# Eighteen constant products at the start of TensorE's program, and six more projection pieces ahead of the first scores

## The chip, the cores and the metric

The kernel runs on one core of a Trainium2 chip. The metric is the device time of one execution in microseconds, as the median of several runs. Lower is better. A core has five engines with a program each, which run side by side and wait for one another by semaphores: TensorE (PE, matrix products; its weight loads are listed apart as PEld), VectorE (DVE), ScalarE (ACT), GpSimd (POOL) and SyncE (SP), which here issues nearly all transfers.

## The reference

One layer of a decoder with 1024 tokens and width 1024. A condition vector gives shifts, scales and gates; the token matrix is modulated, projected, attended in two ways, merged, normalized, and sent through a feed-forward block:

```python
mod = (jnp.einsum('bd,de->be', c_act, w_ada[l]) + b_ada[l])[:, None, :]
shift_m, scale_m, gate_m, shift_f, scale_f, gate_f = jnp.split(mod, 6, axis=-1)
u = x * (1.0 + scale_m) + shift_m
y = mixer(u, positions, w_in[l], sinks[l], w_branch_a[l], w_branch_b[l], w_o[l])
x = layer_norm(DEEPNORM_ALPHA * x + (1.0 + gate_m) * y, ln1_g[l], ln1_b[l])
u = x * (1.0 + scale_f) + shift_f
y = swiglu(u, w_gate_up[l], w_down[l])
x = layer_norm(DEEPNORM_ALPHA * x + (1.0 + gate_f) * y, ln2_g[l], ln2_b[l])
```

The mixer projects `u` by `w_in` (46 column blocks of 128 for queries, keys and values, and 16 for gates), turns queries and keys by rotary tables, runs a sliding-window attention (16 heads) and three dilated attentions (8 heads each), and merges them with sigmoid gates.

## The kernel before

**Tiles.** Everything is float32. Where a large product is needed, each operand is split into a rounded high part and a low rest, and three products (high by high, high by low, low by high; lines 137 to 139) are added up in a PSUM bank of 128 by 512. ACT makes the high part (line 78 for weights, `w_hi`), DVE the rest (line 79, `w_lo`). The modulated input `u` lies in on-chip memory by 8 blocks of 128 features (`k`), two halves of 512 tokens (`t`).

**Prologue** (lines 196 to 367). For each of the 8 feature blocks `j`: the columns of `w_ada` for shift and scale are multiplied by `c_act` and summed over the 1024 condition features. `on_pe[j]` of the 8 partial sums are made by PE (`ada_direct`, line 248, products with one column), the rest by DVE (`ada_sum`, lines 240 and 242, into `acc`). PE then folds `acc` over the partitions with a column of ones (`ada_rest`, line 254). DVE adds the bias (`modulate`, lines 259 and 260, tile `mod`); ACT makes `u` from it (lines 265 and 266), and POOL its low part (line 269). On DVE stands, in this order for every block: `modulate(j)`, `ada_sum(j + 1)`, the low part of an early weight block (line 118), a step of the rotary tables. PE meanwhile multiplies three early weight blocks (blocks 0 to 2; lines 278 and 283) with what there is of `u`. `ones` is a constant of 128 by 128 ones.

**Projection stream and attention** (lines 410 to 775). `stream()` is a generator that yields the projection of blocks 3, 4, ... in pieces: one piece is two feature blocks of one token half, 6 products of 128 by 512; 4 pieces make a half, 8 a column block. A half that is done is taken out of its bank `pj` (two banks) by `evacuate`: for keys and queries DVE does lines 422 and 423 (`ra`, `rb`), POOL lines 425 and 426 (into `r` or `o`); for values ACT copies (line 484). The first attention unit uses the early blocks 0, 1, 2 (key, value, query); blocks 3, 4, 5 are key, value and query of the second unit. After some ticks (one tick a piece, `soon`) a key is split (ACT lines 454 and 455 into `kh`, DVE line 460 into `kl`) and a query likewise (lines 439 and 440, `qs`).

**What sets the order.** The program is written out in one order, and every engine runs its own instructions in that order. The loop at lines 742 to 769 goes over (unit, quarter) steps `s`. Each step issues `scores` (PE lines 501 and 507 into two banks `s`, which the next step uses again; DVE masks and row maxima at lines 513 and 520), pieces up to a count, `turn_probs` of the step before (PE line 550), `exponentials` (ACT line 528), more pieces, and `weigh` (PE line 573). `pump(n)` runs the stream until `n` pieces are done in all. Line 741 is the start: 8 pieces before the first scores; then `at(0.4)`, `at(0.8)` and `at(1.0)` ask for 8, 10 and 12 in step 0, and 14, 16 and 18 in step 1.

Of the kernel before, what the change touches and what calls it, by code (L numbers as in the profile page):

```python
# [10 lines left out]
F32 = mybir.dt.float32  # L11
# [7 lines left out]
P = 128  # L19
# [79 lines left out]
def decoder_layer(ctx: ExitStack, tc: tile.TileContext, I, out, dbg=None):  # L99
    nc = tc.nc  # L100
# [12 lines left out]
    ones = const.tile([P, P], F32, name="ones")  # L113
# [85 lines left out]
    ps_o = ph1.enter_context(tc.tile_pool(name="ps_o", bufs=2, space=PSUM))  # L199
# [18 lines left out]
    with tc.tile_pool(name="pro", bufs=2) as pro:  # L218
# [17 lines left out]
        def ada_sum(j):  # L236

            acc_t[j] = pro.tile([P, 2 * P], F32, name="acc", bufs=2)
            k0 = on_pe[j]
            nc.vector.tensor_scalar(acc_t[j], wa_t[j][:, k0], c_act[:, k0:k0 + 1], None, op0=OP.mult)  # L240
            for k in range(k0 + 1, KC):
                nc.vector.scalar_tensor_tensor(acc_t[j], wa_t[j][:, k], c_act[:, k:k + 1], acc_t[j],
                                               op0=OP.mult, op1=OP.add)

        def ada_direct(j):
            for s in range(2):
                for k in range(on_pe[j]):
                    nc.tensor.matmul(ps_m[:, 2 * j + s:2 * j + s + 1], wa_t[j][:, k, s * P:(s + 1) * P],
                                     c_act[:, k:k + 1], start=(j == 0 and s == 0 and k == 0), stop=False,
                                     skip_group_check=True)  # L250

        def ada_rest(j):
            for s in range(2):
                nc.tensor.matmul(ps_m[:, 2 * j + s:2 * j + s + 1], acc_t[j][:, s * P:(s + 1) * P], ones[:, :1],
                                 start=False, stop=(s == 1), skip_group_check=True)
# [68 lines left out]
        fetch(1)  # L324
        ada_direct(0)
        ada_sum(0)
        ada_rest(0)
        for j in range(KC):
            if j + 2 < KC:
# [41 lines left out]
    def tick():  # L371
        for x in later:
            x[0] -= 1
        for x in [x for x in later if x[0] <= 0]:
            later.remove(x)
            x[1]()
# [326 lines left out]
    ends = np.cumsum(lengths)  # L703
# [3 lines left out]
    def pump(upto):  # L707
        while progress[0] < min(upto, total):
            next(flow)
            progress[0] += 1  # L710
            tick()
# [26 lines left out]

    LEAD = 6
    subs = [(un, qr) for un in units for qr in range(4)]  # L740
    pump(ends[0] + LEAD + 2)
    for s in range(len(subs) + 2):
        n, i = divmod(s, 4)
        start = ends[min(n, len(units) - 1)] + LEAD if n < len(units) else total
        stop = ends[n + 1] + LEAD if n + 1 < len(units) else total
# [555 lines left out]
    f0, ends, nxt = 0, [], 3  # L1301
# [111 lines left out]
```

## Time and profile before

| | us |
|---|---|
| median of 3 runs (1900.1 to 1901.41) | 1901.1 |
| the profiled execution | 1908.77 |
| its span in the trace | 1907.0 |
| PE busy in the span | 1841.1 |
| DVE busy | 1160.4 |
| ACT busy | 782.0 |
| POOL busy | 596.5 |

All moments below are microseconds from the start of the span. The profiled execution was 7.7 us above the median of the timed runs, and 1.77 us of it lie outside the span. PE has work in nearly all of the span; what it lacks lies mostly in the first 100 us. A matmul's length in the trace includes its way through the array, so the pace of a stream is the distance between two starts.

### The profile page before, as it was taken

How to read it: one execution, taken by the hardware profiler on the slowest of the kernel's cores; microseconds unless marked ns; L12 is line 12 of the kernel's file. 1: busy time of each engine (PE TensorE's matmuls, PEld its weight loads, DVE VectorE, ACT ScalarE, POOL GpSimd, SP SyncE). 2: the span in 40 equal slices, each digit the busy share in tenths (PEclk: the TensorE clock that was granted, in tenths of full speed). 3: DMA queues.
4: the chain of work that ended last, by engine and by line, in shares of the span. 5: the costliest groups of instructions: out<-in, count | busy, mean ns of one | idle time of the engine just before them, and what ended most of it. 6: DMA issues, size and time to landing. Idle time of an engine off the chain costs nothing.

```text
span 1907.0 us, 24471 instructions
## 1 busy us (share of the span) xinstructions
PE 1841.1 (97%) x8988; PEld 1489.6 (78%) x8988; DVE 1160.4 (61%) x2161; ACT 782.0 (41%) x1661; POOL 596.5 (31%) x389
## 2 busy tenths in 40 slices
PE   6899999999999999989999999999999999899998
PEld 5688877878878777768888878778888888788886
DVE  7855667667677887534555364575565444565557
ACT  3455545445444767633122132653333333412122
POOL 2432223223323222100311142455664333431213
PEclk9899999999999999989999999999999999999999
DMA  8011112111121122254534123123222222432222
GB/s 316 28 34 34 40 41 74 45 57 56 41 63 50 53 89 68 79 178 164 175 118 161 56 75 124 56 89 100 89 78 89 78 89 95 135 125 90 93 71 89
DMA packets 72266, 170.83 MB, mean 90 GB/s; under 512 B 13073, under 2 KB 14161, under 8 KB 72146
## 3 DMA queue, kind: packets, MB, share of 16 engines
q1 hardware_dynamic: 71810, 168.21, 26.7%
q8 instruction: 71, 1.16, 0.3%
q0 software_dynamic: 336, 1.06, 0.2%
q14 instruction: 49, 0.40, 0.1%
HBM read 145.80 MB, written 23.43 MB: 89 GB/s over the span
## 4 chain that ended last, share of the span: by engine, by line
PE 51%; DVE 3%; ACT 1%; issue 1%; DMA 1%; SPq 0%; POOL 0%; DVEq 0%; ACTq 0%; POOLq 0%
PE pf L1106 21%; PE p L138 5%; PE p L139 5%; PE p L137 5%; PE pf L137 5%; PE pf L139 5%; PE pf L138 5%; DVE m L118 1%; DMA h_raw<-h_d 0%; DVE wd L79 0%; DVE h L118 0%; DMA oa_d<-o 0%; PE px L1034 0%; PE p L835 0%; PE p L842 0%
## 5 line engine op out<-in xcount | busy, mean ns | idle before, releaser
L137 PE MATMUL pj<-u,w_hi 128*128 128x512 f32 x720 | 301.5, 419 | 0.0
L139 PE MATMUL pj<-u,w_lo 128*128 128x512 f32 x720 | 283.9, 394 | 0.0
L138 PE MATMUL pj<-u,w_hi 128*128 128x512 f32 x720 | 282.6, 392 | 0.0
L425 POOL TENSOR_TENSOR rb<-rb,sin_t 128x512 f32<-128x512 f32 x64 | 86.8, 1356 | 502.0 <-DVE rb L423 431.5
L118 DVE TENSOR_TENSOR w_lo<-r,w_hi 128x512 fp32r<-128x512 f32 x110 | 117.7, 1072 | 138.7 <-ACT w_hi L117 137.9
L79 DVE TENSOR_TENSOR w_lo<-w_raw,w_hi 128x512 fp32r<-128x512 f32 x150 | 133.4, 893 | 85.3 <-ACT w_hi L78 83.0
L528 ACT ACTIVATE probs<-probs,st 128x128 f32<-128x128 f32 (+1 forms) x320 | 146.0, 461 | 60.5 <-DVE st L518 30.8
L137 PEld LDWEIGHTS pj<-u,w_hi 128*128 128x128 f32 x720 | 136.4, 189 | 33.6 <-issue 4.7
L139 PEld LDWEIGHTS pj<-u,w_lo 128*128 128x128 f32 x720 | 135.8, 189 | 30.7
L138 PEld LDWEIGHTS pj<-u,w_hi 128*128 128x128 f32 x720 | 136.7, 190 | 22.6
L137 PE MATMUL pf<-wd,h 128*128 128x512 f32 x352 | 139.2, 395 | 3.4 <-DVE zt L1326 2.9
L138 PE MATMUL pf<-wd,h 128*128 128x512 f32 x352 | 138.7, 394 | 1.9 <-DVE wd L79 1.9
L139 PE MATMUL pf<-wd,h 128*128 128x512 f32 x352 | 138.6, 394 | 0.0
L62 POOL TENSOR_TENSOR w_raw<-w_raw,gate 128x512 f32<-128x512 f32 x60 | 83.1, 1404 | 157.0 <-DMA w_raw<-in_w_down 134.4
L1326 DVE SCALAR_TENSOR_TENSOR zt<-zt,pf 128x512 f32<-128x512 f32 x112 | 76.2, 685 | 85.1 <-PE pf L139 85.0
L426 POOL TENSOR_TENSOR r<-ra,rb 128x512 f32<-128x512 f32 x63 | 114.5, 1817 | 6.1 <-DVE kl L460 1.3
L78 ACT ACTIVATE w_hi<-w_raw 128x512 fp32r<-128x512 f32 x150 | 92.0, 624 | 29.0 <-PE p L138 12.0
L552 ACT ACTIVATE ptsb<-pt 128x512 f32<-128x512 f32 (+1 forms) x128 | 63.6, 548 | 93.6 <-PE pt L550 93.2
L137 PE MATMUL p<-u,w_hi 128*128 128x512 f32 x224 | 88.3, 394 | 0.0
L139 PE MATMUL p<-u,w_lo 128*128 128x512 f32 x224 | 87.2, 389 | 0.0
L138 PE MATMUL p<-u,w_hi 128*128 128x512 f32 x224 | 87.2, 389 | 0.0
L137 PE MATMUL p<-o_hl,w_hi 128*128 128x512 f32 x192 | 75.9, 395 | 8.0 <-ACT o_hl L117 8.0
(297 smaller groups left out, 4267.2 us busy)
## 6 DMA issues: line engine op xcount, KB each, us to landing
w_raw<-in_w_in SPq DMA_DIRECT2D x118, 256.0 KB
r<-in_w_gate_up SPq DMA_DIRECT2D x47, 512.0 KB
a_raw<-in_w_ada SPq DMA_DIRECT2D x32, 512.0 KB
w_raw<-in_w_down SPq DMA_DIRECT2D x44, 256.0 KB
h_raw<-h_d SPq DMA_DIRECT2D x22, 512.0 KB
h_d<-g SPq DMA_DIRECT2D x40, 256.0 KB
wa<-in_w_ada_m SPq DMA_DIRECT2D x16, 512.0 KB
wb<-wt_d SPq DMA_DIRECT2D x24, 256.0 KB
```

Source lines behind the costliest of these rows:

```text
L62: self.nc.gpsimd.tensor_tensor(self.raws[i], self.raws[i], scale(), op=OP.mult)
L78: self.nc.scalar.activation(hi, raw, AF.Copy)
L79: self.nc.vector.tensor_tensor(lo, raw, hi, op=OP.subtract)
L118: nc.vector.tensor_tensor(lo, src, hi, op=OP.subtract)
L137: nc.tensor.matmul(ps, w[0], m[0], start=first, stop=False)
L138: nc.tensor.matmul(ps, w[0], m[1], start=False, stop=False)
L139: nc.tensor.matmul(ps, w[1], m[0], start=False, stop=last)
L425: eng.tensor_tensor(b, b, sin_t[:, s], op=OP.mult)
L426: eng.tensor_tensor(residue_half(res, r, t), by_residue(a, r), by_residue(b, r), op=OP.add)
L528: nc.scalar.activation(pr, pr, AF.Exp, bias=st[:, 0, h, b:b + 1], accum_out=st[:, 1, h, b:b + 1])
L1106: nc.tensor.matmul(ps, w[:, c], m[:, k], start=first and k == 0 and n == 0, stop=k == 3 and n == 2, skip_group_check=True)
L1326: nc.vector.scalar_tensor_tensor(z, z, ALPHA if gi == 0 else 1.0, pd, op0=OP.mult, op1=OP.add)
```

## The change

Two edits. At the start of the prologue, between `ada_direct(0)` with `ada_sum(0)` and `ada_rest(0)`, 18 products of `ones` by `ones` are written to a bank of the pool `ps_o`; nothing reads them. And the count of pieces ahead of the first scores goes from 8 to 14. The later counts are the same, so the requests for 8, 10, 12 and 14 pieces then find nothing left to do.

```diff
@@ -324,6 +324,10 @@
         fetch(1)
         ada_direct(0)
         ada_sum(0)
+
+        idle = ps_o.tile([P, P], F32, name="po")
+        for _ in range(18):
+            nc.tensor.matmul(idle, ones, ones, start=True, stop=True)
         ada_rest(0)
         for j in range(KC):
             if j + 2 < KC:
@@ -738,7 +742,7 @@
 
     LEAD = 6
     subs = [(un, qr) for un in units for qr in range(4)]
-    pump(ends[0] + LEAD + 2)
+    pump(ends[0] + LEAD + 8)
     for s in range(len(subs) + 2):
```

In the changed kernel every line from 328 on has a number that is higher by 4 (501 becomes 505, 513 becomes 517, and so on). On PE, at the very start of the program, the difference between the two orders is this; `acc` is the sum that DVE makes, `pt` the bank of the modulation:

```order
-L1409 UNCONDITIONAL_BRANCH
+L1413 UNCONDITIONAL_BRANCH
 L248 MATMUL pt<-c_act,wa 128x1 x8
+L330 MATMUL po<-ones 128x128 x18
 L254 MATMUL pt<-ones,acc 128x1 x4
 L296 MATMUL s<-pos_f,ones 128x512 x2
```

The 18 products stand behind the 8 products of `ada_direct(0)` and ahead of the first `ada_rest`, on which `modulate(0)` waits.

On PE around the first scores, before; `s` are the scores, `pj` the projection, `probs` the masked scores of the first quarter. A line of "..." stands for the products of the pieces between (24 between the two scores, 12 behind the second):

```order
L501 MATMUL s<-kh,qs 128x128 x2
L501 MATMUL s<-kh,qs 128x256 x2
L507 MATMUL s<-kl,qs 128x128 x2
L507 MATMUL s<-kl,qs 128x256 x2
...
L501 MATMUL s<-kh,qs 128x256 x4
L507 MATMUL s<-kl,qs 128x256 x4
...
L550 MATMUL pt<-ident,probs 128x128 x6
```

And in the changed kernel, with nothing left out between them:

```order
L505 MATMUL s<-kh,qs 128x128 x2
L505 MATMUL s<-kh,qs 128x256 x2
L511 MATMUL s<-kl,qs 128x128 x2
L511 MATMUL s<-kl,qs 128x256 x2
L505 MATMUL s<-kh,qs 128x256 x4
L511 MATMUL s<-kl,qs 128x256 x4
L554 MATMUL pt<-ident,probs 128x128 x6
```

The 36 products of six pieces moved ahead of the first scores; the scores of the first two quarters and the turning of the first `probs` now follow each other directly.

On DVE, from the query's split to the first masks, before (`kl` here is the low part of the second unit's key, block 3):

```order
L440 TENSOR_TENSOR qs<-o,qs 64x1024 x2
L422 TENSOR_TENSOR ra<-pj,cos_t 128x512
L423 STREAM_SHUFFLE rb<-pj 128x512
L513 ISA probs,mx<-s,mask 128x128
```

And in the changed kernel:

```order
L444 TENSOR_TENSOR qs<-o,qs 64x1024 x2
L426 TENSOR_TENSOR ra<-pj,cos_t 128x512
L427 STREAM_SHUFFLE rb<-pj 128x512
L464 TENSOR_TENSOR kl<-r,kh 64x1024
L79 TENSOR_TENSOR w_lo<-w_raw,w_hi 128x512
L464 TENSOR_TENSOR kl<-r,kh 64x1024
L79 TENSOR_TENSOR w_lo<-w_raw,w_hi 128x512
L517 ISA probs,mx<-s,mask 128x128
```

Four instructions that stood behind the first masks (the first three of them between the masks of the first and of the second quarter) stand ahead of both now. ACT moved in the same way: the four copies of that key (lines 454 and 455), two `w_hi` and a copy of `vt` stand ahead of the first exponentials instead of behind them.

## Rows read from the trace of the kernel before

**Rows 1.** Page, busy time: us, share of the span, instructions.

```profile
PE 1841.1 (97%) x8988; PEld 1489.6 (78%) x8988; DVE 1160.4 (61%) x2161; ACT 782.0 (41%) x1661; POOL 596.5 (31%) x389
```

**Rows 2.** Stretches: from:to, length, busy by engine (columns in the head), clock, DMA.

```profile
core 0: us, PE busy (x) PEld busy (x) DVE busy (x) ACT busy (x) POOL busy (x), PEclk, DMA share, GB/s
13.00:55.50 42.50, 33.53 (x120) 25.23 (x120) 40.87 (x65) 17.33 (x22) 15.63 (x12) 0.96 0.77 281
70.00:93.00 23.00, 15.81 (x74) 12.68 (x72) 22.45 (x30) 9.87 (x11) 10.50 (x7) 0.87 0.08 24
90.00:100.00 10.00, 8.82 (x29) 6.91 (x30) 7.01 (x16) 4.47 (x11) 3.41 (x2) 0.63 0.00 0
```

**Rows 3.** Timeline, PE at the start: start, length, line, names, count [idle before <-releaser].

```profile
6.43 3.55 PE L248 MATMUL pt<-c_act,wa 128*128 128x1 f32 x16 [6.43 <-DMA wa<-in_w_ada_m]
9.83 0.99 PE L254 MATMUL pt<-ones,acc 128*128 128x1 f32 x4
18.62 1.01 PE L254 MATMUL pt<-ones,acc 128*128 128x1 f32 x4 [7.80 <-DVE acc L242]
```

**Rows 4.** Timeline, DVE in the prologue and behind it.

```profile
10.90 0.16 DVE L259 TENSOR_TENSOR mod<-pt,b_pp 128x2 f32<-128x2 f32 x1 [1.34 <-PE pt L254]
...
12.81 0.35 DVE L240 TENSOR_SCALAR acc<-wa,c_act 128x256 f32<-128x256 f32 x1 [1.55 <-DMA wa<-in_w_ada_m]
...
70.11 0.69 DVE L422 TENSOR_TENSOR ra<-pj,cos_t 128x512 f32<-128x512 f32 x1 [2.56 <-PE pj L283]
```

**Rows 5.** Timeline, later products with a whole float32 operand.

```profile
891.46 0.19 PEld L835 LDWEIGHTS p<-acc,ones 128*128 128x128 f32 x1 [0.24 <-issue]
...
948.13 1.84 PE L842 MATMUL p<-ones,acc 128*128 128x1 f32 x16
```

**Rows 6.** Timeline, PE, two of the early products of the prologue.

```profile
29.35 0.63 PE L278 MATMUL s<-u,e_hi 128*128 128x512 f32 x1
29.78 0.63 PE L278 MATMUL s<-u,e_lo 128*128 128x512 f32 x1
```

**Rows 7.** Timeline, PE around the first two scores.

```profile
83.38 0.39 PE L138 MATMUL pj<-u,w_hi 128*128 128x512 f32 x1
83.61 0.39 PE L139 MATMUL pj<-u,w_lo 128*128 128x512 f32 x1
90.38 0.45 PE L501 MATMUL s<-kh,qs 128*128 128x128 f32 x1 [6.38 <-DVE qs L440]
91.63 0.98 PE L501 MATMUL s<-kh,qs 128*128 128x128 f32 x3 [0.81 <-DVE qs L440]
92.54 0.79 PE L507 MATMUL s<-kl,qs 64*128 64x128 f32 x4
...
97.27 0.46 PE L137 MATMUL pj<-u,w_hi 128*128 128x512 f32 x1
...
104.62 0.81 PE L550 MATMUL pt<-ident,probs 128*128 128x128 f32 x6
105.19 0.48 PE L137 MATMUL pj<-u,w_hi 128*128 128x512 f32 x1
```

**Rows 8.** Timeline, DVE around the first masks.

```profile
92.13 0.72 DVE L423 STREAM_SHUFFLE rb<-pj 128x512 f32<-128x512 f32 x1
93.37 0.29 DVE L513 CUSTOM_DVE_ANT_0 probs<-s,mask 128x128 f32<-128x128 f32 x1 [0.52 <-PE s L507]
...
94.82 1.62 DVE L520 TENSOR_SCALAR st<-mx 128x2 f32<-128x2 f32 x1
98.44 1.22 DVE L460 TENSOR_TENSOR kl<-r,kh 64x1024 fp32r<-64x1024 f32 x1 [2.00 <-ACT kh L454]
100.18 0.69 DVE L79 TENSOR_TENSOR w_lo<-w_raw,w_hi 128x512 fp32r<-128x512 f32 x1 [0.52 <-ACT w_hi L78]
```

**Rows 9.** Timeline, POOL, the second half of block 3.

```profile
94.29 2.12 POOL L426 TENSOR_TENSOR r<-ra,rb 128x512 f32<-128x512 f32 x1
```

**Rows 10.** Timeline, ACT, first and last of seven instructions on end.

```profile
97.37 1.04 ACT L454 ACTIVATE kh<-r 64x1024 fp32r<-64x1024 f32 x1
...
102.82 0.63 ACT L78 ACTIVATE w_hi<-w_raw 128x512 fp32r<-128x512 f32 x1
```

## The prediction

> **What bounds the kernel now.** The page comes first: PE is busy for 97% of the span [rows 1], so any time that PE loses without work is time of the kernel, and a gain can only come from a gap. The waits of PE are then looked up in its timeline. There are two in the first 100 us that matter here. At the start PE has no gap where the 18 products go: its first `ada_rest` starts at 9.83, while the products of `ada_direct(0)` still drain; the long wait of 7.80 us comes one `ada_rest` later, for DVE's second sum [rows 3]. The other gap is in front of the first scores: the last product starts at 83.61, and PE then stands for 6.38 and 0.81 us until the query's split on DVE is there [rows 7].
>
> In both stretches the engine to look at is DVE. From 13 to 55.5 it is busy for 40.87 of 42.5 us, from 70 to 93 for 22.45 of 23 [rows 2]. The prologue is DVE's chain, started by its second sum at 12.81, and DVE's first rotary step at 70.11 follows the end of that prologue [rows 4]. What delays the second sum delays all behind it.
>
> **The 18 products.** Each counts as two rows in the trace: the 8 of `ada_direct(0)` are the x16 of [rows 3]. So 36 rows are added, on PE, in front of `ada_rest(0)`. No row shows a 128 by 128 float32 product of this kind, so it is bounded. Loading 128 columns and streaming one takes 3.55 / 16 = 0.222 us a row at that place [rows 3], and 1.84 / 16 = 0.115 us late in the kernel [rows 5]. Streaming 512 columns takes 0.19 + 0.24 = 0.43 us there [rows 5], so 128 take 0.107, and twice that at the low clock: early products start 0.43 us apart [rows 6], late ones of the same shape 0.23 [rows 7], the 1.2 and the 2.4 GHz level (the clock column, 0.96 for 13 to 55.5 [rows 2], does not show this early low level, the pace does). Load and stream run side by side, since busy PE and busy PEld add up to far more than the span [rows 1]; the dearer of the two counts. That gives 36 x 0.115 = 4.1 us if PE is at the high level throughout, and 36 x 0.25 = 9.0 at the pace of the first `ada_rest`, 0.99 / 4 [rows 3]. I take the low level for as long as it lasted after the stall at the scores, from 91.63 to the shortened row at 97.27, 5.6 us [rows 7], in a stretch with a granted clock of 0.63 [rows 2]: 25 rows of 0.222, then 11 of 0.115, 6.9 us.
>
> `ada_rest(0)` starts that much later, and with it `mod` at 10.90. The cover is small: DVE waited 1.55 us for the second block's transfer behind `modulate(0)` [rows 4]. So DVE's second sum slips by 6.9 - 1.55 = 5.3 us (2.6 to 7.5). Nothing in the prologue gives it back: DVE has 1.6 us without work in 42.5 [rows 2]. SP's transfers are released by the same sums and slip with them; ACT, POOL and the early products on PE wait for `mod`. First term: +5.3 us.
>
> **The six pieces.** All moments here are without the slip, which carries DVE, PE, ACT and POOL alike. The 36 products follow 83.61 at 0.23 each, 8.2 us, so by count they would fill the 7.2 us of waiting. But only the first 24 can run at once. The other 12 write the second `pj` bank, and this is freed by line 423 at 92.13 + 0.72 = 92.85, behind the query's split on DVE [rows 8]. PE stands from about 89.3 to 92.9, then needs 2.7 to 5.1 us for the 12, by level. The first scores end between 96.6 and 99.8, against 93.3 before.
>
> Then comes the larger loss. The masks of these scores now stand behind two `kl` and two `w_lo` on DVE. The `kl` are the split of block 3's key; its data leave POOL at 94.29 + 2.12 = 96.41 [rows 9]. ACT's seven instructions from the first key copy to the second `w_hi` took from 97.37 to 102.82 + 0.63, 6.08 us [rows 10]; before, they began 0.96 us after POOL, since ACT was busy with exponentials, which now come later. They begin at 96.45 and end at 102.5; the last `w_lo` (0.69) ends at 103.2, and the masks start there, where they started at 93.37 [rows 8]. They need 1.5 us until the second bank `s` is read (93.37 to 94.82), so the second scores, which nothing separates from the first any more, start at 104.7. PE stands for 5 to 8 us a second time. At the low level the second scores take some 1.8 us (the first, smaller ones took 1.7 from 91.63) and the six turns of line 550 twice the 0.57 between 104.62 and 105.19: the next piece starts at 107.6, against 105.19 [rows 7], 2.4 us later with the same work done on both sides. PE then stays low until 104.7 + 5.6 = 110.3 and loses 47% of 2.7 us, 1.3. Second term: +3.7 us. At the high level throughout it is 104.7 + 0.9 + 0.6, +1.0; above, I allow 5.0, for a low level that lasts 2.8 us longer.
>
> **Sum.** 5.3 + 3.7 = +9.0 us. The profiled execution of 1908.77 (span 1907.0) would become 1917.8. The durations are those of that execution, 7.7 us above the median of the runs; added to the median the sum gives 1901.1 + 9.0 = 1910.1. The ends are 2.6 + 1.0 = +3.6 and 7.5 + 5.0 = +12.5, so 1904.7 to 1913.6 for this case.
>
> **Rivals.** (a) *The gap is filled after all.* Place: DVE between the query's split and the masks. If the first masks came right behind the first scores, as before, PE at the high level would end them at 96.6, the masks at 98.1, the second scores at 99.1, the turns at 99.8: 5.4 us earlier than 105.19, which pays for the products: 5.3 - 5.4 = -0.1, 1901.0; with cheap products (2.6) 1898.3. It decides from the point where the masks start before about 98. For it speaks that the count of 36 products fits the gap; against it that DVE, with masks or not, sat idle 2.00 us for the key copy at 98.44 with work behind it [rows 8].
> The Trainium skill, "TensorE: Matmul & The Clock Gate", Part 1, Architectural detail, says that VectorE's queue is a strict first-in, first-out one and only TensorE's pulls loads ahead; by that rule (a) cannot happen with this order, and the idle 2.00 us agree.
>
> (b) *The products cost nothing.* If in other executions the second block's transfer lands some 5 us later than at 12.81, DVE waits for it anyway. Then only the second term stays: +3.7, 1904.8. For it: that wait exists; against: it is 1.55 us.
>
> (c) *A warmed PE pays back.* The products could leave PE at the high level, so that the early products from 23 to 32 us run at 0.23 instead of 0.43: 20 of them save some 4 us, and the sum is 5.3 - 4.0 + 3.7 = +5.0, 1906.1. Against it: PE would wait from the end of the products to the second sum, over 5 us without work, and in that stretch DVE sets the pace [rows 2], so PE's speed is not what is waited for.
> The Trainium skill, same page, "Why this matters for your kernels", advises matmuls ahead of the measured ones so that those run at the full clock. The rows agree that the early products run at the low level. By the rule the time would be (c)'s, by DVE's row the forecast's; the page also warns of idle gaps behind such a burst, which the 5 us are.
>
> **How the numbers follow.** Forecast 0.79, (a) 0.08, (b) 0.08, (c) 0.05. 0.2% (3.8 us) is about what a measurement of this kernel tells from no change. Faster needs (a) with cheap products: 0.06. The same takes the rest of (a), (b), whose 1904.8 lies just inside, and little of the forecast's low end: 0.12. Slower: 0.82. The forecast's own range is 1904.7 to 1913.6; with the rivals' side and a low level that lasts longer than I assume, 1902.5 to 1914.5.
>
> **What would show it.** In the changed profile: 36 rows of line 330 from about 9.9 to 14 to 19, and `mod` of the first block right behind; DVE's second sum without a wait for DMA before it, and later than 12.81 by 2.6 to 7.5; the first rotary step at 70.11 plus the same amount. PE's wait in front of the first scores gone from `qs` and found again in two places: a product of the fifth extra piece waiting for `rb` (some 3.5 us), and the second scores waiting for the masks of the first (5 to 8 us). The masks behind `w_lo`, near 103.2 plus the slip. I am wrong if the second sum starts near 12.8, or if PE has no wait above 3 us between the first scores and the first turn, or if the shift at 105 us shrinks later.

## The result and the profile after

The changed kernel took 1907.78 us (median of 6 runs, 1906.13 to 1910.06) against 1901.03 for the kernel before in the same comparison: 6.75 us more. The ratio, 1.0038 with a 95% interval of 1.0029 to 1.0048, comes from the single executions and is not the quotient of these two medians (1.0036). By it the change costs 7.2 us (5.5 to 9.1). It is slower, as forecast; the forecast was 1910.1 and +9.0. One of the eight executions of a later run, the one with the products alone, took 3677.97 us; it counts in that run's median (1904.90 without it) but not in its ratio.

The profiled execution of the changed kernel has a span of 1905.2 us, less than the 1907.0 of the first profile of before, an execution 7.7 us above its median. So these two spans can't be compared. A second profile of the kernel before was taken for that (`e0_control` below, span 1897.4), and the shifts are measured between moments inside the programs.

At the start of the changed kernel, TensorE's timeline (columns as in [rows 3]) shows the 36 rows of line 330 ahead of the first fold of line 254:

```profile
5.84 3.55 PE L248 MATMUL pt<-c_act,wa 128*128 128x1 f32 x16 [5.84 <-DMA wa<-in_w_ada_m]
9.25 6.80 PE L330 MATMUL po<-ones 128*128 128x128 f32 x36
15.89 0.50 PE L254 MATMUL pt<-ones,acc 128*128 128x1 f32 x4
22.51 1.01 PE L254 MATMUL pt<-ones,acc 128*128 128x1 f32 x4 [6.12 <-DVE acc L242]
```

They need 15.89 - 9.25 = 6.64 us. The fold (the four-row product of line 254) that started at 9.83 [rows 3] starts at 15.89, and the long wait behind it is still there, 6.12 us. DVE's timeline in the same stretch, with its first rotary step as the last row:

```profile
16.43 0.16 DVE L259 TENSOR_TENSOR mod<-pt,b_pp 128x2 f32<-128x2 f32 x1 [7.43 <-PE pt L254]
...
16.70 0.34 DVE L240 TENSOR_SCALAR acc<-wa,c_act 128x256 f32<-128x256 f32 x1
...
73.28 0.69 DVE L426 TENSOR_TENSOR ra<-pj,cos_t 128x512 f32<-128x512 f32 x1 [2.56 <-PE pj L283]
```

DVE waits 7.43 us for the first fold instead of 1.34; the second sum no longer waits for a transfer [rows 4]. The same rows of the second profile of before:

```profile
11.73 0.35 DVE L240 TENSOR_SCALAR acc<-wa,c_act 128x256 f32<-128x256 f32 x1 [0.86 <-DMA wa<-in_w_ada_m]
...
68.35 0.69 DVE L422 TENSOR_TENSOR ra<-pj,cos_t 128x512 f32<-128x512 f32 x1 [2.56 <-PE pj L283]
```

Against these, the second sum slips by 4.97 us and the rotary step by 4.93: in this pair the prologue gives nothing back. Around the first scores, TensorE's timeline of the changed kernel:

```profile
96.11 0.50 PE L137 MATMUL pj<-u,w_hi 128*128 128x512 f32 x1 [3.06 <-DVE rb L427]
...
100.55 0.62 PE L505 MATMUL s<-kh,qs 128*128 128x128 f32 x4
101.10 0.50 PE L511 MATMUL s<-kl,qs 64*128 64x128 f32 x4
107.06 0.58 PE L505 MATMUL s<-kh,qs 128*128 128x256 f32 x1 [5.46 <-DVE mx L517]
...
109.47 1.54 PE L554 MATMUL pt<-ident,probs 128*128 128x128 f32 x6
110.67 0.77 PE L137 MATMUL pj<-u,w_hi 128*128 128x512 f32 x1
...
113.37 0.48 PE L137 MATMUL pj<-u,w_hi 128*128 128x512 f32 x1
```

The wait of 6.38 us for `qs` [rows 7] is gone. In its place stand 3.06 us for the bank `pj` and 5.46 us for the masks. Why the masks are late is read on DVE and on ACT. DVE, columns as above:

```profile
100.73 1.22 DVE L464 TENSOR_TENSOR kl<-r,kh 64x1024 fp32r<-64x1024 f32 x1 [4.68 <-ACT kh L458]
102.47 0.69 DVE L79 TENSOR_TENSOR w_lo<-w_raw,w_hi 128x512 fp32r<-128x512 f32 x1 [0.52 <-ACT w_hi L78]
103.55 1.22 DVE L464 TENSOR_TENSOR kl<-r,kh 64x1024 fp32r<-64x1024 f32 x1 [0.38 <-ACT kh L458]
105.76 0.69 DVE L79 TENSOR_TENSOR w_lo<-w_raw,w_hi 128x512 fp32r<-128x512 f32 x1 [0.99 <-ACT w_hi L78]
106.37 0.28 DVE L517 CUSTOM_DVE_ANT_0 probs<-s,mask 128x128 f32<-128x128 f32 x1
```

and POOL's half of the key with ACT's first and last instruction of the chain:

```profile
97.49 2.12 POOL L430 TENSOR_TENSOR r<-ra,rb 128x512 f32<-128x512 f32 x1
```

```profile
99.64 1.06 ACT L458 ACTIVATE kh<-r 64x1024 fp32r<-64x1024 f32 x1 [14.13 <-POOL r L430]
...
105.10 0.63 ACT L78 ACTIVATE w_hi<-w_raw 128x512 fp32r<-128x512 f32 x1
```

The masks of the first quarter start at 106.37, though the scores were there at about 101.6. Ahead of them DVE sat idle for 4.68 + 0.52 + 0.38 + 0.99 us, for ACT, which itself had waited 14.13 us for POOL. The chain of [rows 8 to 10] now stands in front of the masks instead of behind them. The masks start 13.0 us later than in [rows 8].

The clock column, for the same stretches of the changed kernel (from:to, length, busy by engine, clock, DMA):

```profile
13.00:55.50 42.50, 33.79 (x135) 25.99 (x133) 37.62 (x61) 15.16 (x19) 14.26 (x10) 0.80 0.75 274
90.00:100.00 10.00, 6.83 (x22) 4.87 (x21) 6.00 (x6) 0.36 (x1) 5.79 (x3) 0.83 0.08 28
100.00:115.00 15.00, 9.38 (x39) 7.32 (x38) 7.06 (x24) 11.69 (x26) 0.00 (x0) 0.66 0.11 36
```

From 100 to 115 us TensorE has work for 9.38 of 15 us at a granted clock of 0.66. That is a mean of the high level (1.00, 2.4 GHz) and the low one (0.50, 1.2 GHz); from 107.06 to 113.37, behind the wait for the masks, the column says 0.50.

### The profile page after: what moved, and what is told of

It is laid out like the page before. It is cut to its first block, busy times and chain, and to the rows that moved or that the text cites. A ratio compares the mean times of both kernels' runs of the same rounds, so it can differ in the third digit from the quotient of the medians.

```text
span 1905.2 us, 24545 instructions
## 1 busy us (share of the span) xinstructions
PE 1843.1 (97%) x9024; PEld 1492.5 (78%) x9024; DVE 1159.9 (61%) x2161; ACT 782.0 (41%) x1661; POOL 597.1 (31%) x389
## 4 chain that ended last, share of the span: by engine, by line
PE 50%; DVE 3%; ACT 1%; DMA 1%; issue 1%; POOL 0%; SPq 0%; DVEq 0%; ACTq 0%; POOLq 0%
PE pf L1110 21%; PE p L138 5%; PE p L139 5%; PE p L137 5%; PE pf L137 5%; PE pf L139 5%; PE pf L138 5%; DVE m L118 1%; DMA h_raw<-h_d 0%; DVE wd L79 0%; DVE h L118 0%; DMA oa_d<-o 0%; PE px L1038 0%; PE p L839 0%; PE p L846 0%
```

## The experiments

Two theories stood against each other for the loss. The one of the prediction: two terms that add, the products through DVE's prologue and the pieces through the masks' place on DVE. Against it: one edit costs it all and the other is neutral. Ten kernels were run; each ratio is to executions of the kernel before in the same comparison, and a loss or gain given below with an interval is worked out from the ratio. "Shift" is how much later or earlier than in `e0_control` (127.4 us; 129.4 in the first profile of before) the first product of line 573 starts, in the one profile of each run; it sums up all that happened until then. The two profiles of the kernel before differ by 2.1 us there, so a shift of up to 2 us need not come from the edit.

| run | what | median, us | ratio, 95% interval | shift, us |
|---|---|---|---|---|
| e0_control | before again | 1900.62 | 0.9999 (0.9990 to 1.0008) | 0 |
| changed kernel | both edits | 1907.78 | 1.0038 (1.0029 to 1.0048) | +8.9 |
| e1_products | products alone | 1905.09 | 1.0022 (1.0011 to 1.0032) | +5.3 |
| e2_pieces | pieces alone | 1904.98 | 1.0025 (1.0014 to 1.0035) | +4.1 |
| e3_products_later | products one place later | 1899.41 | 0.9998 (0.9989 to 1.0007) | +0.5 |
| e9_products_36 | 36 products alone | 1908.63 | 1.0044 (1.0029 to 1.0060) | +8.9 |
| e4_pieces_split_later | 14 pieces, key split later | 1900.53 | 0.9996 (0.9987 to 1.0004) | -0.2 |
| e6_eight_split_later | 8 pieces, key split later | 1902.07 | 1.0007 (0.9998 to 1.0016) | +1.0 |
| e5b_twelve_split_later | 12 pieces, key split later | 1899.15 | 0.9991 (0.9983 to 1.0000) | -2.1 |
| e5c_twelve_ahead | 12, and 4 more in step 0 | 1896.36 | 0.9973 (0.9962 to 0.9984) | -3.3 |
| e8_twelve_ahead_split8 | the same, split later still | 1894.67 | 0.9967 (0.9955 to 0.9980) | -6.0 |

**The kernel before again.**

> The kernel before, once more, for a second profile of it. The first profiled execution of before took 1908.77 us, 7.7 above its median; the changed kernel's profile took 1906.98, 0.8 below its own. Theory: those 7.7 us of the first profile lie late (behind 800 us) and are of that execution alone. Then this profile is near 1901 to 1903, with the first 110 us as before: first rotary step on DVE near 70.1, first masks near 93.4, the piece behind the first turns near 105.2, and the same work late in the kernel some 5 us or more earlier than in the first profile. Rival: a profile always costs some 7 us, then it is near 1908 again. Times: ratio 1.000.

The profiled execution took 1899.17 us. A profile does not cost 7 us; the first one was a long execution, mostly late in the kernel: the two profiles differ by 1.8 us at the first rotary step (68.35, where 70.1 had been expected), by 2.1 at line 573 and by 9.6 at the end. One part of it is early: the second input block came 12.81 - 6.43 = 6.4 us behind the first product [rows 3, 4], here 11.73 - 6.09 = 5.6.

**The products alone.**

```diff
-    pump(ends[0] + LEAD + 8)
+    pump(ends[0] + LEAD + 2)
```

> The 18 products alone, 8 pieces ahead of the first scores as before. Theory (two terms that add): only DVE's prologue slips. In the changed kernel its first rotary step came 3.2 us later than before, with the first input block 0.6 us earlier: +3.2 to +3.8 us, about 1904.5; the wait in front of the first scores stays at 6.4 plus 0.8 us and the first masks come right behind the scores. Rival 1 (the pieces cost it all and the products are absorbed): 1901.0. Rival 2 (the products cost it all): +6.75, 1907.8.

+4.2 us (2.1 to 6.1). Both rivals lie outside; the theory's 3.2 to 3.8 lies inside. Its first rotary step stands at 73.58, 5.2 us behind `e0_control`, and the first scores wait as before. TensorE, the profile of this run:

```profile
93.85 0.44 PE L505 MATMUL s<-kh,qs 128*128 128x128 f32 x1 [6.38 <-DVE qs L444]
95.10 0.98 PE L505 MATMUL s<-kh,qs 128*128 128x128 f32 x3 [0.81 <-DVE qs L444]
```

The same 6.38 and 0.81 us as in [rows 7], 3.5 us later than there and 5.2 later than in `e0_control` (88.61): the whole stretch is shifted and not changed.

**The pieces alone.** The change without its first hunk.

> The 14 pieces alone, no constant products. Theory: second term only. First rotary step at 70.1 as before; the wait for the query's split gone; some 3 us of waiting for the bank pj and some 5.5 us for the masks instead; masks at 103.2; the piece behind the first turns at 107.6; +3.7 us in all, about 1904.7. Rival 1: +6.75, 1907.8. Rival 2: +0, 1901.0.

+4.75 us (2.7 to 6.7), where +3.7 had been expected; of the rivals, 0 lies outside and 6.75 just so. TensorE waits in the two places where it waits in the changed kernel, 3.06 us for the bank and 4.23 instead of 5.46 for the masks:

```profile
91.86 0.79 PE L137 MATMUL pj<-u,w_hi 128*128 128x512 f32 x1 [3.06 <-DVE rb L423]
...
102.81 0.58 PE L501 MATMUL s<-kh,qs 128*128 128x256 f32 x1 [4.23 <-DVE mx L513]
```

DVE's first rotary step and first masks in this run, and the first masks in `e0_control`:

```profile
69.03 0.69 DVE L422 TENSOR_TENSOR ra<-pj,cos_t 128x512 f32<-128x512 f32 x1 [2.56 <-PE pj L283]
...
102.12 0.28 DVE L513 CUSTOM_DVE_ANT_0 probs<-s,mask 128x128 f32<-128x128 f32 x1
```

```profile
91.60 0.29 DVE L513 CUSTOM_DVE_ANT_0 probs<-s,mask 128x128 f32<-128x128 f32 x1 [0.51 <-PE s L507]
```

The masks stand 33.1 us behind the first rotary step; in `e0_control` 91.60 - 68.35 = 23.3, so 9.8 later. The two runs add up to 8.9 us; the change measured 7.2 (5.5 to 9.1). Within the intervals the terms add, and both rivals fall.

**The products one place later.**

```diff
         ada_rest(0)
+        idle = ps_o.tile([P, P], F32, name="po")
+        for _ in range(18):
+            nc.tensor.matmul(idle, ones, ones, start=True, stop=True)
         for j in range(KC):
```

> The 18 products one place later on PE, behind the first fold of DVE's sum (line 254), in the 7.80 us that PE waited there; 8 pieces as before. Theory: they cost nothing, since the second fold waits for DVE until 18.6 and the products end near 17.5; DVE's second sum stays near 12.8, the first rotary step at 70.1 or up to 0.7 earlier through a faster PE late in the prologue: 0 to -0.7 us, 1900.3 to 1901.1. Rival (a warmed PE pays back): the early products run at 0.23 instead of 0.43 us and PE's speed is what is waited for: -4, 1897. Rival (the products cost by themselves, for example through the power budget of the clock): +3, 1904.

-0.4 us (-2.1 to 1.3): no difference that can be told. The cost of the products is their place ahead of the first fold, not the products. They don't pay either: TensorE, the profile of this run:

```profile
10.88 5.71 PE L330 MATMUL po<-ones 128*128 128x128 f32 x36
18.00 0.60 PE L254 MATMUL pt<-ones,acc 128*128 128x1 f32 x4 [1.42 <-DVE acc L242]
...
20.81 0.63 PE L278 MATMUL pj<-u,e_lo 128*128 128x512 f32 x1
21.23 0.63 PE L278 MATMUL pj<-u,e_hi 128*128 128x512 f32 x1
25.07 1.01 PE L254 MATMUL pt<-ones,acc 128*128 128x1 f32 x4 [2.79 <-DVE acc L242]
```

The fold at 18.00 is quick (0.60 instead of 1.01, the granted clock 1.00 from 14.0 to 20.7), but from 20.8 on the early products are 0.42 us apart, the low level (0.50 from 20.8 to 31.0), as in [rows 6]; and the fold at 25.07 waits 2.79 us for DVE. In `e0_control` the same fold waited less:

```profile
24.70 1.02 PE L254 MATMUL pt<-ones,acc 128*128 128x1 f32 x4 [0.43 <-DVE acc L242]
```

What TensorE gained by the products it lost again in waiting for DVE.

**Twice as many products.** `range(36)` instead of `range(18)` in the run with the products alone.

> The constant products alone, twice as many (36), 8 pieces as before. Theory: the first 18 use up the cover of DVE's wait for the second input block, so that every further row counts in full, 36 more rows of some 0.11 us at the high level: DVE's second sum near 21 instead of 17, +4 us on the run with 18, +8 against before, about 1909. Rival (PE waits after the products in any case, and only the first ones cost): +4 as with 18, 1905.

+8.4 us (5.5 to 11.4). TensorE, the profile of this run:

```profile
9.26 10.71 PE L330 MATMUL po<-ones 128*128 128x128 f32 x72
19.80 0.50 PE L254 MATMUL pt<-ones,acc 128*128 128x1 f32 x4
```

The first 18 took 6.64 us in the changed kernel, the next 18 19.80 - 9.26 - 6.64 = 3.9: 0.109 us a row, all of which DVE's second sum pays (20.61 instead of 16.70), as the theory has it.

**14 pieces, with block 3's key split later.** `e == 3` is that key; a tick is one piece.

```diff
-                soon(2 + h + (2 if e < EARLY else 0), lambda h=h: stack(res, h))
+                soon(2 + h + (2 if e < EARLY else 6 if e == 3 else 0), lambda h=h: stack(res, h))
...
-    pump(ends[0] + LEAD + 2)
+    pump(ends[0] + LEAD + 8)
```

> 14 pieces ahead of the first scores, no constant products, and the split of block 3's key called 6 ticks later, so that its kl and kh stand behind the masks and exponentials of the first two quarters. Theory (the second term is the masks' place behind kl and w_lo): first and second scores follow each other with a wait of 1 to 2 us instead of 4.2; the wait of 3.1 us for the bank pj and the low clock behind it stay; masks near 98 instead of 102 to 103, the first turns near 101 instead of 105; later the copy of vt stands behind two key copies on ACT and costs PE up to 1.6 us: -2 us against before, about 1899. Rival (the bank pj and the low clock cost it, not the masks): as the pieces alone, +4, 1905.

The 4.75 us of the pieces are gone (-0.8, -2.5 to 0.8), with the wait for the bank still there: it was the masks' place. TensorE, the profile of this run, waits 0.73 and 0.36 us for them instead of 4.23:

```profile
91.51 0.79 PE L137 MATMUL pj<-u,w_hi 128*128 128x512 f32 x1 [3.06 <-DVE rb L423]
...
98.83 0.39 PE L501 MATMUL s<-kh,qs 128*128 128x256 f32 x1 [0.73 <-DVE mx L513]
99.58 0.63 PE L501 MATMUL s<-kh,qs 128*128 128x256 f32 x3 [0.36 <-DVE mx L513]
100.57 1.42 PE L550 MATMUL pt<-ident,probs 128*128 128x128 f32 x6
```

The gain of 2 us was not reached. The first turns come 2.3 us earlier than in `e0_control` (both against their first rotary step), but the turns take 1.1 us instead of 0.6, and the three pieces behind them, from 101.64 to 107.02, 5.4 instead of 4.2: the first five products there run at the low level, behind the waits for the bank and for the masks.

**8 pieces, with the key split later.** The first line of that diff alone.

> 8 pieces as before, no constant products, only block 3's key split 6 ticks later: what the later split does by itself. Theory: nothing in front of the first scores changes (waits of 6.4 and 0.8 us stay); 0 to +1.6 us through the wait for vt behind the key copies on ACT, 1901 to 1902.6. Rival (the later split is a gain by itself, and the runs with more pieces live from it): -2 or more, 1899.

+1.3 us, with an interval that holds none (-0.4 to +3.0), and the expected new wait, 1.04 us for `vt` in front of line 480. The later split is no gain by itself, so what the run with 14 pieces won back came from the masks.

**12 pieces.** As with 14, but `LEAD + 6`, and 4 instead of 6 ticks.

> 12 pieces ahead instead of 14, so that no piece ahead of the scores writes the second bank pj, and block 3's key split 4 ticks later; no constant products. Theory: PE waits some 2.3 us for the query's split instead of 7.2, then some 2.4 for the masks between first and second scores, and up to 1.8 for vt on ACT; no wait for the bank; the turns end near 99.3 instead of 105.2: -4 us, about 1897. Rival (what is taken from this gap comes back in others): 0, 1901.

-1.7 us (-3.2 to 0) and not -4. The waits around the scores are short (0.61, 0.95, 1.39 and 0.76 us). TensorE, the second scores and what follows them:

```profile
92.75 0.38 PE L501 MATMUL s<-kh,qs 128*128 128x256 f32 x1 [1.39 <-DVE mx L513]
93.89 1.01 PE L501 MATMUL s<-kh,qs 128*128 128x256 f32 x3 [0.76 <-DVE mx L513]
...
96.15 0.63 PE L138 MATMUL pj<-u,w_hi 128*128 128x512 f32 x1
96.58 0.63 PE L139 MATMUL pj<-u,w_lo 128*128 128x512 f32 x1
```

With little work between the waits TensorE fell to the low level (granted clock 0.50 from 95.56 to 100.10), 0.43 us a product: the two pieces behind the second scores took from 95.56 to 100.53, 5.0 us where 2.7 were expected. This suggests that the wait for the masks needs cover, not only a shorter gap ahead; the next run puts it there.

**12 pieces and cover between the scores.** The same, and in step 0 every request is 4 higher, so that four pieces lie between the first two scores again:

```diff
-        at = lambda x: pump(min(int(start + (stop - start) * (i + x) / 4), total - 1))
+        more = 4 if s == 0 else 0
+        at = lambda x: pump(min(int(start + (stop - start) * (i + x) / 4) + more, total - 1))
```

> As the run with 12 pieces and the later split, but the first step asks for 4 pieces more than before, so that four pieces lie between the first and the second scores as in the kernel before and cover the masks. Theory: only the wait of some 2.3 us in front of the first scores and up to 1 us for vt are left; with 16 pieces done the second turns come some 6 to 7 us earlier than before: -6.5 us, about 1894.5. Rival (what is taken from this gap comes back in others): 0, 1901.

-5.1 us (-7.2 to -3.0), where -6.5 had been expected. Cover without the later split of the key was not run. Left of TensorE's waits are 0.61 and 0.95 us in front of the first scores, 0.27 for the bank, and one of 1.85 us in front of line 480, for `ptsb` (the turned probabilities, line 552), which stood on ACT behind the four key copies.

**The same, with the key split 8 ticks later.** `8 if e == 3` instead of `4 if e == 3`.

> As the run with 12 pieces and 4 more in the first step, but block 3's key is split 8 instead of 4 ticks later, so that on ACT its four copies stand behind the first ptsb copies and the second exponentials. Theory: the wait of 1.85 us for ptsb in front of the vt turns, and the low clock behind it, go; waits of some 1.6 us in front of the first scores stay: 2 to 3 us faster than that run (1896.4), -7 against before, about 1894. Rival (the key is then late for something else, such as the rotary of block 5 that writes the same tile): no gain on that run, 1896 or more.

-6.3 us (-8.6 to -3.8), 1894.67 us: 1.2 us better than the run ahead of it, where 2 to 3 had been expected, and well within both intervals. In TensorE's waits between 70 and 120 us (us in total, times, longest), the 1.85 is gone:

```profile
PE s L501 <- DVE qs L440: 1.6, 2, 1.0
PE pt L550 <- DVE v L481: 0.4, 1, 0.4
PE pj L137 <- DVE rb L423: 0.3, 1, 0.3
```

2.3 us of waiting, where the kernel before has 7.2 [rows 7] and the changed kernel 8.7. This version beats both in time.

## Why the prediction was right

- **The bound.** Two gaps of TensorE, both set by DVE: confirmed by the run with the products alone (the gap in front of the scores moves whole) and by the one with the later split.
- **Price of the products.** 6.9 us by 25 rows at the low and 11 at the high level (these terms add up to 6.8); measured 6.64, and 0.109 us a row at the high level where 0.115 was taken. 24 rows at 0.222 and 12 at 0.109 would give the 6.64, an estimate from these rows.
- **Slip of the second sum.** +5.3 predicted. Against `e0_control` it is 4.97 at the sum and 4.93 at the first rotary step; against [rows 4] it is 3.9 and 3.2. From the first product of the program it is 5.2 in the pair with `e0_control` (16.70 - 5.84 against 11.73 - 6.09), and there two errors cancel: the cover of 1.55 us was that of one execution (0.86 in the second profile), and the fold at the high level was 0.5 us quicker, which was left out. So the near hit is in part luck. In the eight profiles without constant products the first rotary step stands between 68.05 and 70.11, the middle at 68.8; with the 18 products it stands at 73.28 and 73.58, so 4.5 to 4.8 behind the middle. The first term came out somewhat too high.
- **Nothing given back.** It held against `e0_control`: 56.6 us from the second sum to the first rotary step in both. But that time itself differs by execution: 57.3 to 57.4 in the first profile of before and in five of the runs without the products (granted clock 0.83 from 46 to 56 us), 56.6 in `e0_control` and in the run with 8 pieces and the later split (1.00). The 0.7 us go with the clock late in the prologue in all these profiles; no run was made to test it.
- **The bank.** A wait of some 3.5 us at the fifth extra piece; 3.06 measured, and the low level behind it.
- **The masks.** 103.2 without the slip. From the first rotary step to the masks it is 33.1 us, and 23.3 in [rows 4, 8] as in the second profile of before: 9.8 us later, as predicted (93.37 to 103.2).
- **The second term.** +2.4 at the piece behind the first turns, +3.7 when the clock is back. From the first rotary step to that piece: 110.67 - 73.28 = 37.4, in `e0_control` 103.12 - 68.35 = 34.8: +2.6. Here too two deviations cancel: the second scores began 0.7 us behind the start of the masks where 1.5 had been taken, and took 2.4 us to the first turns where 1.8 had been. To the second turns: 122.36 - 73.28 = 49.1, in `e0_control` 113.44 - 68.35 = 45.1: +4.0. TensorE was at the low level for 6.3 us from 107.06 to 113.37, 5.6 had been taken.
- **The sum.** +9.0 predicted, +8.9 at line 573 against `e0_control`, and in time 6.75 by the medians and 7.2 by the ratio (5.5 to 9.1). The prediction had named it as a sign of being wrong that the shift shrinks later. The times do not decide that, since 8.9 lies inside their interval. In the pair of traces it does shrink, to 7.8 us at the end of the span, and most of it in one wait, for the first split of line 117 behind the attention. TensorE in the changed kernel, then in `e0_control`:

```profile
846.08 0.80 PE L137 MATMUL p<-o_hl,w_hi 128*128 128x512 f32 x1 [6.56 <-ACT o_hl L117]
```

```profile
838.70 0.80 PE L137 MATMUL p<-o_hl,w_hi 128*128 128x512 f32 x1 [7.77 <-ACT o_hl L117]
```

The shift is 8.6 us ahead of this wait and 7.4 behind it. Over all profiles, of every version, the wait ranges from 6.0 to 8.0. Whether the change itself shortens it, or single executions differ by that much, stays open. That a shift of the first 100 us reaches the end in full was taken without a row for it.
- **Rivals.** (a) fell: DVE sat idle for ACT with masks behind. The strict order of VectorE's queue that the Trainium skill states ("TensorE: Matmul & The Clock Gate", Part 1, Architectural detail) agrees with that. (b) fell: the transfer's cover was 0.56 to 1.55 us in the profiles where DVE waits for it, and with the 18 products DVE waited over 7 us for the first fold in both profiles. (c) fell by the run with the products one place later: no gain that can be told, where the rival had 4 us. The advice of the Trainium skill (same page, "Why this matters for your kernels") to run matmuls ahead of the measured ones agrees with the rows that follow at once (the first fold took 0.50 instead of 0.99). Behind a wait the rows differ: in the changed kernel the fold behind 6.12 us was slow again (1.01); in the run one place later the fold and the products of line 296 behind 1.42 us were still quick (0.60 and 1.98 us instead of 1.01 and 3.77), and the early products behind them were not.

## What to carry to other kernels

Work that is written ahead of a gap moves with it everything that it triggers on the other engines; look in the order of those engines for what now stands ahead of the instruction that ends the gap. A filler belongs behind the instruction that another engine waits for, not ahead of it, and a gap is worth only as much work as has its buffers free. When pieces are moved from between two dependent steps to ahead of both, the second wait loses its cover: here the moved order paid most (5.1 and 6.3 us against 1.7) when the same number of pieces stayed between, in runs in which the key was split later too.

## What had not been expected of the hardware

The early low level is not in the clock column. In the changed kernel the column says 1.00 from 9.3 to 14.5 us, where 25 rows of the constant products took the 5.2 us, about twice the 0.109 us a row of later ones. In `e0_control` it says 1.00 from 22 to 30 us, with early products 0.43 us apart. In the changed kernel, behind the quick end of the constant products, it says 0.50 from 21.5 to 35.0 us. In these traces a low level shows only after the clock has risen once.

Short waits were followed by a fall where little work lay between them: in the run with 12 pieces four waits of 0.61 to 1.39 us within 5.4 us came ahead of two pieces at half pace. In the last version, with four pieces between the first two scores, waits of 0.60, 0.95 and 0.27 us were followed by none (granted clock 1.00 from 89 to 100 us).
